# SiLU behind three weight copies, and one down piece split between the two halves of the gate

## The chip, the cores and the metric

The kernel runs on one core of one Trainium2 chip. Its time is that of one execution on the device in microseconds (us); lower is better. PE is the matrix engine (TensorE), DVE the vector engine (VectorE), ACT the scalar engine (ScalarE), POOL GpSimd, SP the queue that issues most DMAs.

## The reference, cut to what matters

One layer of a bidirectional encoder on 1024 tokens of width 1024: an adaLN norm, differential attention, then a mixture of 16 experts of width 512, of which each token uses two, and a last norm. The change lies in the experts:

```python
hid = silu(t @ w_gate) * (t @ w_up)      # per expert: 1024 -> 512, twice
hid = hid * gates                        # weight of the token for this expert
y = hid @ w_down                         # 512 -> 1024, summed over experts
x = x + g2 * y
```

## The kernel before, in words

Attention and routing fill the first part of the run. The experts e = 0 to 15 then follow one after the other, each in a call of `block`. An expert gathers its tokens. The first 128 go through the main path; if it has more, up to 64 further ones go through a second, smaller path (`small_gate`, `small_up`, `small_hid`, `small_down`), which stands under a branch at run time.

Float32 products are made of pairs: a value is kept as a high part (fp32r) and the rest (low), and a product is the sum of three matmuls, high x high, high x low and low x high. So each weight has to be split on chip. An expert's weights are 12 pieces of 128 x 1024 values: pieces 0 to 3 belong to the gate product, 4 to 7 to the up product, 8 and 9 to the first half of the down product, 10 and 11 to its second. A piece is loaded by a DMA on SP into one of 11 raw tiles, copied by ACT into its high part (`split_hi`, L1115), and DVE subtracts that from the raw piece to get the low part (`split_lo`, L1120). After the split the raw tile is free and the load of the piece 11 places later is issued (`split_done`, `raw_to`). High and low parts lie in a ring of 14 slots.

ACT, DVE, POOL and PE work in exactly the order in which the program names their instructions (`manual_schedule`). What stands beside the matmuls is put in place by hooks: a hook (c, what) is issued just before matmul number c of the block, and `upto(c)` issues all that are due by c. For experts 1 to 15 the list `SPL` sets pieces 4, 5 and 6 at c = 0, 8 and 16, and pieces 7, 8 and 9 at c = 24, 32 and 40. Expert 0 has pieces 8 to 11 in a list of its own (`SP0`), the last two at c = 30 and 40.

In a block, PE does the gate product (24 matmuls, c = 0 to 23), then the up product for the first 6 of 8 row groups (18 matmuls, c = 24 to 41), then the last two row groups in two halves of 256 columns (6 short matmuls each). ACT takes SiLU of the gate columns (`silu`, L1385). DVE multiplies SiLU, the token's weight and the up columns for each half (`gated`, L1391); the second half's matmuls wait for the first half's `gated`, since both halves lie in one PSUM tile. Eight small DVE instructions that build a one-hot matrix for expert e + 2 (L1228, hook c = 46) stand ahead of the first `gated`; experts 14 and 15 have none. Then PE transposes the next expert's tokens (L1274) and the gated columns (`hid`, L1428), ACT and DVE split these (L1431, L1432), and PE does the down product in two halves (L1441); the second half's transposes stand after six matmuls of the first. Before the change `splits(11)`, that is the split of piece 10, stands after the first `hid`, and pieces 11, 12 and 13 (the last two are the next expert's first two) follow by `splits(14)`, both ahead of the second `hid` on ACT and DVE.

Of the kernel before, what the change touches and what calls it, by code (L numbers as in the profile page):

```python
# [15 lines left out]
P = 128  # L16
S = 1024
D = 1024
KT = D // P
# [16 lines left out]
def build(tc, x, c, ada_w, ada_b, norm_mix, norm_ffn, w_in, lq1, lk1, lq2, lk2, subln, w_out,  # L36
# [1098 lines left out]
    def split_to(n):  # L1135
        while nsplit[0] < min(n, NE * NP):
            split_piece(*divmod(nsplit[0], NP))
            split_done(1)
# [143 lines left out]
    def small_pt():  # L1282
        return mps.tile([P, KT, M2], F32, name="xt", bufs=2)
# [13 lines left out]
    def run(g):  # L1297
        try:
            while True:
                next(g)  # L1300
        except StopIteration as r:
            return r.value
# [33 lines left out]
    def finish15(ix, py, yo, xc):  # L1336
        sq = ss_tile()
        for i in range(2):
            h = slice(i * 512, (i + 1) * 512)
            v.tensor_tensor(yo[:, h], py[i], g2b[:, h], op=OP.mult)  # L1340
            v.tensor_tensor(xc[:, h], xc[:, h], yo[:, h], op=OP.add)
            nc.scalar.activation(py[i], xc[:, h], AF.Square, accum_out=sq[:, i:i + 1])
            if i == 0:
                nc.scalar.activation(sq[:, 0:1], sq[:, 0:1], AF.Identity, scale=1.0 / D, bias=epst)
        v.tensor_tensor(yo, xc, nfin[0], op=OP.mult)
        r = sq[:, 1:2]
        nc.scalar.activation(r, r, AF.Ln, scale=1.0 / D, bias=sq[:, 0:1])
        nc.scalar.activation(r, r, AF.Exp, scale=-0.5)
        nc.scalar.activation(yo[:, 0:512], yo[:, 0:512], AF.Copy, scale=r)
        v.tensor_scalar(yo[:, 512:1024], yo[:, 512:1024], r, None, op0=OP.mult)  # L1350
        out_rows(ix, yo)
# [19 lines left out]
    def gu_tile():  # L1371
        return mps.tile([P, 512], F32, name="gu", bufs=2)

    def gu(e, XT, i, R, pg, ks=range(KT), n=slice(0, 512)):

        for k in ks:
            for xi, wi in TERMS[R]:
                yield
                w = WP[e, i * 4 + k // 2][wi].rearrange("p (k n) -> p k n", k=2)
                nc.tensor.matmul(pg[:, n], XT[:, xi, k], w[:, k % 2, n], start=(k == 0 and xi == 0 and wi == 0),  # L1380
                                 stop=(k == KT - 1 and (xi, wi) == TERMS[R][-1]), skip_group_check=True)

    def silu(pg):
        sl = mp.tile([P, 512], F32, name="sl")
        nc.scalar.activation(sl, pg, AF.Silu)  # L1385
        return sl

    def gated(sl, pu, g, hf):

        n = slice(hf * 256, hf * 256 + 256)  # L1390
        v.scalar_tensor_tensor(sl[:, n], sl[:, n], g, pu[:, n], op0=OP.mult, op1=OP.mult)  # L1391
        return sl[:, n]
# [32 lines left out]
    def hid(sl, R, name="hid", bufs=2, hT=None):  # L1425
        ph = mps.tile([P, 2, P], F32, name="tp")
        for i in range(2):
            nc.tensor.transpose(ph[:, i, :R], sl[:R, i * P:(i + 1) * P], ident[:R, :R])  # L1428
        hT = mp.tile([P, 2, 2, P], F32R, name=name, bufs=bufs) if hT is None else hT
        hi, lo = hT[:, 0], hT[:, 1]  # L1430
        nc.scalar.copy(hi, ph[:, :, :R])  # L1431
        v.tensor_tensor(lo, ph[:, :, :R], f(hi), op=OP.subtract)  # L1432
        return hT

    def down(e, py, hf, hT, R, ns=(0, 1)):
        terms = [(i, xi, wi) for i in range(2) for xi, wi in TERMS[R]]
        terms.sort(key=lambda t: t[1])
        for n in ns:
            for j, (i, xi, wi) in enumerate(terms):
                yield  # L1440
                nc.tensor.matmul(py[n], hT[:, xi, i], WP[e, 8 + hf * 2 + i][wi][:, n * 512:(n + 1) * 512],  # L1441
                                 start=(hf == 0 and j == 0), stop=(hf == 1 and j == len(terms) - 1), skip_group_check=True)

    def take(g, n):
        for _ in range(n):
            next(g, None)
# [25 lines left out]
    def small15(XT, ix, g):  # L1472

        e, R, xs = NE - 1, M2, XG[NE - 1, 1]
        small_evac(small_pe(xs), XT)
        xc = raw_tile()
        acc_rows(ix, xc[:R])
        small_gate(e, XT, gu_tile(), xs)
        small_up(e, XT, gu_tile(), xs, g)
        hs = mp.tile([P, 2, 2, P], F32R, name="hs")  # L1480
        small_hid(xs, hs)
        small_down(e, [mps.tile([P, 512], F32, name="spy%d" % n, tag="xt", bufs=2) for n in range(2)], hs, xs)
        xc, yo = xc[:R], xs[:R]
        v.tensor_tensor(xc, xc, yo, op=OP.add)
        sq = ss_tile()[:R]
        nc.scalar.activation(yo, xc, AF.Square, accum_out=sq[:, 0:1])
        r = rstd_of(sq, R)
        v.scalar_tensor_tensor(xc, xc, r, nfin[0][:R], op0=OP.mult, op1=OP.mult)
        out_rows(ix, xc)
# [28 lines left out]
    def block(e, XT, idx, tt, hooks):  # L1518


        count = [0]
        ix = idx[:, 0:1]
        last = e == NE - 1
        hooks = sorted(hooks, key=lambda hk: hk[0])
        py = [mps.tile([P, 512], F32, name="py%d" % i) for i in range(2)]

        def upto(c):
            while hooks and hooks[0][0] <= c:
                hooks.pop(0)[1]()

        def go(g, n=1 << 30):
            try:
                for _ in range(n):
                    next(g)
                    upto(count[0])
                    count[0] += 1
            except StopIteration as r:
                return r.value

        def splits(k):  # L1540

            split_to(e * NP + k)

        g1 = tt[:, 0, 1:2]
        pg, pu = gu_tile(), gu_tile()
        go(gu(e, XT, 0, P, pg))
        st = silu(pg)
        go(gu(e, XT, 1, P, pu, range(KT - 2)))
        sl = []
        for hf in range(2):  # L1550
            go(gu(e, XT, 1, P, pu, range(KT - 2, KT), slice(hf * 256, hf * 256 + 256)))
            sl.append(gated(st, pu, g1, hf))
        upto(99)
        if last:
            h0 = hid(sl[0], P)
            splits(NP)
            run(down(e, py, 0, h0, P))
            upto(150)
            h1 = hid(sl[1], P)
            nc.scalar.preload_act_table_set("natural_log_exp_and_others")  # L1560
            upto(1 << 30)
            run(down(e, py, 1, h1, P))
            finish15(ix, py, mp.tile([P, D], F32, name="yo"), XC[0])
            tc.no_sync_barrier()
            with tc.If(cnts[e] > P, label="small"):
                small15(XT, idx[:M2, 1:2], tt[:, 1, 1:2])
            tc.no_sync_barrier()
            with tc.If(cnts[NE] > P + M2):
                rest(XT)
            return  # L1570
        n = cnts[e]
        g = tt[:, 1, 1:2]
        xs = XG[e, 1]

        def small(what):
            tc.no_sync_barrier()
            with tc.If(n > P):  # L1577
                what()

        def evac():  # L1580
            yo = mp.tile([P, D], F32, name="yo")
            for n in range(2):
                v.tensor_tensor(yo[:, n * 512:(n + 1) * 512], py[n], g2b[:, n * 512:(n + 1) * 512], op=OP.mult)
            scatter_add(ix, yo)

        pt = small_pt()
        small(lambda: small_evac(small_pe(xs, pt), XT))

        upto(XPH)
        h0 = hid(sl[0], P)  # L1590

        upto(SMM)
        splits(11)
        sg, su = gu_tile(), gu_tile()
        small(lambda: small_gate(e, XT, sg, xs))
        splits(14)
        d = down(e, py, 0, h0, P)
        take(d, 6)
        h1 = hid(sl[1], P)
        run(d)  # L1600
        small(lambda: small_up(e, XT, su, xs, g))
        splits(15)
        run(down(e, py, 1, h1, P))
        if e == NE - 2:
            evac()
        hs = mp.tile([P, 2, 2, P], F32R, name="hs")
        spy = [mps.tile([P, 512], F32, name="spy%d" % n, tag="xt", bufs=2) for n in range(2)]

        def small_d():
            small_down(e, spy, hs, oyo)  # L1610
            scatter_add(idx[:M2, 1:2], oyo[:M2])

        small(lambda: small_hid(xs, hs))
        splits(16)
        later.append((DSM if e < NE - 2 else 4, lambda: small(small_d)))
        if e < NE - 2:
            later.append((EVAC, evac))
        upto(1 << 30)
# [14 lines left out]
    XT = run(xpose(XG[0, 0]))  # L1633
# [22 lines left out]
    for e in range(NE):  # L1656
# [46 lines left out]
        if e + 1 < NE:  # L1703
# [4 lines left out]
            XT = xp[0]  # L1708
# [34 lines left out]
```

## Time and profile before

| | before |
|---|---|
| median of 3 runs | 1269.76 us (1265.92 to 1269.80) |
| profiled execution, its own time | 1267.65 us |
| its span | 1265.9 us |
| mean granted TensorE clock | 0.945 of full speed |
| busy share of the span: PE, DVE, ACT, POOL | 89%, 74%, 57%, 20% |
| experts 0 to 14, SiLU of expert 0 to SiLU of expert 15 | 455.24 us |

Read a row of the timeline as: start in us from the span's start, duration in us, engine, line, operation, output and inputs, number of instructions merged into it, and in brackets how long the engine had been idle before it and what it waited for. "whi" and "wlo" are the high and low parts of a weight piece, "wraw" the raw piece, "gu" the PSUM tiles of gate and up, "sl" the SiLU tile, "py" the down product. A row of the windows view gives a stretch, its length, the busy us and number of instructions of PE, PE's weight loads, DVE, ACT and POOL, then the granted clock as a share of full speed (1.00 is 2.4 GHz, 0.50 is 1.2 GHz), the mean busy share of the DMA engines and what they moved in GB/s; its last line sums the stretches asked for. A matmul's duration includes what overlaps the next one; the starts give the rate.

### The profile page before, as it was taken

The page shows a single profiled execution, that of the slowest core. Times are in us where ns is not written, and L with a number is a line of the kernel's source. Part 1 is how long each engine was busy: PE and PEld are TensorE (multiplying, and loading weights), DVE is VectorE, ACT ScalarE, POOL GpSimd, SP SyncE. Part 2 cuts the span into 40 slices and gives each one's busy share as a digit, 9 for nine tenths or more (in the row PEclk, how much of TensorE's full clock was granted, in tenths as well). Part 3 has the DMA queues.
Part 4 walks back from the last instruction along what each step waited for, and adds up shares of the span by engine and source line. Part 5 has one row for each costly group of instructions (what it writes and reads, how often), then busy time and mean ns, then how long its engine had stood idle before and what let it go on. Part 6 is the DMA issues. An engine that isn't in the chain of part 4 may idle for free. (4 is left out here: it accounts for less than half of the span.)

```text
span 1265.9 us, 17489 instructions
## 1 busy us (share of the span) xinstructions
PE 1126.6 (89%) x5896; PEld 891.1 (70%) x5896; DVE 941.7 (74%) x1548; ACT 722.3 (57%) x1178; POOL 259.5 (20%) x250
## 2 busy tenths in 40 slices
PE   4989999999999999998999969888989888988990
PEld 3657777777777787776778857666767666777770
DVE  5868788898889677779755577767667778576774
ACT  5556766666677676767644235545455565454553
POOL 3011110111111020125024123212112223122122
PEclk8999999999999999998999979888989989898996
DMA  9622032323223110125058347877776878667745
GB/s 329 193 67 63 25 102 81 98 84 90 82 83 92 34 38 16 36 76 162 25 182 289 124 142 276 267 274 234 230 245 200 269 260 292 220 207 219 223 137 232
DMA packets 120479, 199.41 MB, mean 158 GB/s; under 512 B 12967, under 2 KB 58696, under 8 KB 120370
## 3 DMA queue, kind: packets, MB, share of 16 engines
q1 hardware_dynamic: 113664, 179.86, 42.2%
q0 software_dynamic: 6512, 17.68, 5.9%
q8 instruction: 53, 0.87, 0.3%
q10 hardware_dynamic: 194, 0.54, 0.2%
q14 instruction: 56, 0.46, 0.1%
HBM read 175.77 MB, written 27.67 MB: 161 GB/s over the span
## 5 line engine op out<-in xcount | busy, mean ns | idle before, releaser
L1120 DVE TENSOR_TENSOR wlo<-wraw,whi 128x1024 fp32r<-128x1024 f32 x187 | 224.2, 1234 | 63.2 <-ACT whi L1115 47.3
L1380 PE MATMUL gu<-whi,XT 128*128 128x512 f32 (+1 forms) x672 | 220.6, 391 | 32.8 <-DVE sl L1391 30.1
L486 ACT ACTIVATE E<-E,mn 128x1024 f32<-128x1024 f32 x128 | 147.1, 1151 | 85.1 <-DVE mn L483 84.6
L1115 ACT CAST whi<-wraw 128x1024 fp32r<-128x1024 f32 x192 | 191.5, 1046 | 6.4 <-DMA wraw<-in_expert_w_gate 1.4
L1380 PEld LDWEIGHTS gu<-whi,XT 128*128 128x128 f32 x672 | 128.9, 195 | 69.4 <-DVE sl L1391 33.3
L483 DVE CUSTOM_DVE_ANT_0 E<-S,negd 128x1024 f32<-128x1024 f32 x128 | 152.8, 1219 | 18.2 <-PE S L478 17.6
L1380 PE MATMUL gu<-wlo,XT 128*128 128x512 f32 (+1 forms) x384 | 149.5, 389 | 0.0
L285 PE MATMUL mm<-hH,wh 128*128 128x512 f32 x336 | 139.3, 415 | 2.1 <-DVE V L384 2.1
L285 PE MATMUL mm<-hL,wh 128*128 128x512 f32 x336 | 140.2, 417 | 0.0
L285 PE MATMUL mm<-hH,wl 128*128 128x512 f32 x336 | 138.8, 413 | 0.0
L143 POOL TENSOR_TENSOR wl<-wraw,wh 128x1024 fp32r<-128x1024 f32 x21 | 50.6, 2410 | 325.8 <-ACT wh L142 255.7
L513 ACT CAST aH<-tp 128x512 fp32r<-128x512 f32 x128 | 74.0, 578 | 72.8 <-PE tp L511 72.5
L1441 PE MATMUL py<-whi,hid 128*128 128x512 f32 x256 | 97.4, 434 | 14.8 <-ACTq L1577 5.8
L497 DVE SCALAR_TENSOR_TENSOR E<-E,r 128x1024 f32<-128x1024 f32 x64 | 85.8, 1340 | 27.8 <-ACT E L495 26.3
L514 DVE TENSOR_TENSOR aL<-tp,aH 128x512 fp32r<-128x512 f32 x128 | 87.9, 687 | 17.5 <-ACT aH L513 16.3
L511 PE MATMUL tp<-ident,E 128*128 128x128 f32 x512 | 78.8, 277 | 10.8 <-DVE aL L514 7.4
L511 PEld LDWEIGHTS tp<-ident,E 128*128 128x128 f32 x512 | 62.6, 142 | 34.3 <-DVE aL L514 14.4
L1380 PEld LDWEIGHTS gu<-wlo,XT 128*128 128x128 f32 x384 | 76.1, 198 | 14.6
L693 PE MATMUL mm<-wo,wh 128*128 128x512 f32 x240 | 80.0, 408 | 1.3 <-ACT mm L705 1.3
L285 PEld LDWEIGHTS mm<-hH,wh 128*128 128x128 f32 x336 | 63.5, 189 | 18.2 <-issue 5.1
L285 PEld LDWEIGHTS mm<-hH,wl 128*128 128x128 f32 x336 | 63.5, 189 | 17.1 <-issue 7.9
L285 PEld LDWEIGHTS mm<-hL,wh 128*128 128x128 f32 x336 | 63.3, 189 | 16.9 <-issue 8.0
(341 smaller groups left out, 2230.8 us busy)
## 6 DMA issues: line engine op xcount, KB each, us to landing
wraw<-in_expert_w_gate SPq DMA_DIRECT2D x64, 512.0 KB
wraw<-in_expert_w_up SPq DMA_DIRECT2D x64, 512.0 KB
wraw<-in_expert_w_down SPq DMA_DIRECT2D x64, 512.0 KB
aw<-in_ada_w SPq DMA_DIRECT2D x64, 256.0 KB
wraw<-in_attn_w_in SPq DMA_DIRECT2D x23, 512.0 KB
ld<-in_ada_w SPq DMA_DIRECT2D x32, 256.0 KB
ld<-in_x SPq DMA_DIRECT2D x8, 512.0 KB
xt<-in_x SPq DMA_DIRECT2D x8, 512.0 KB
```

The costliest lines, as they stand in the source:

```text
L285: nc.tensor.matmul(pq, w[:, k], t[k][:, n], start=(k == 0 and i == 0), stop=(k == KT - 1 and i == 2))
L483: nc.vector.tensor_tensor_reduce(out=e, in0=sps[m], in1=negd[:, w0:w0 + S], op0=OP.add, op1=OP.min, scale=-slope, scalar=3.0e38, accum_out=mn)
L486: nc.scalar.activation(e, e, AF.Exp, bias=mn, scale=-1.0, accum_out=sm)
L497: nc.vector.scalar_tensor_tensor(es[0], es[1], r2, es[0], op0=OP.mult, op1=OP.add)
L511: nc.tensor.transpose(pt[:, i], a[:, k * P:(k + 1) * P], ident)
L513: nc.scalar.copy(th[:, kk * 4:kk * 4 + 4, q], pt)
L514: nc.vector.tensor_tensor(tl[:, kk * 4:kk * 4 + 4, q], pt, f(th[:, kk * 4:kk * 4 + 4, q]), op=OP.subtract)
L693: nc.tensor.matmul(py, w[:, h], wt[h][:, ns], start=(h == 0 and s == 0), stop=(h == H - 1 and s == 2))
L1115: nc.scalar.copy(WP[e, i][0], RAW[e, i])
L1120: eng.tensor_tensor(low, RAW[e, i], f(high), op=OP.subtract)
L1380: nc.tensor.matmul(pg[:, n], XT[:, xi, k], w[:, k % 2, n], start=(k == 0 and xi == 0 and wi == 0), stop=(k == KT - 1 and (xi, wi) == TERMS ...
L1441: nc.tensor.matmul(py[n], hT[:, xi, i], WP[e, 8 + hf * 2 + i][wi][:, n * 512:(n + 1) * 512], start=(hf == 0 and j == 0), stop=(hf == 1 and ...
```

## The change

In the source, SiLU of the gate columns moves from ahead of the up product's first 18 matmuls to behind them. On PE nothing moves. On ACT, in experts 1 to 15, SiLU now stands behind the copies of pieces 7, 8 and 9; in expert 0 behind those of pieces 10 and 11. `upto(40)` issues nothing that was not issued already. The split of piece 10 moves from after the first `hid` to between the first and the second `gated`: its copy on ACT, its subtraction on DVE, and on SP the load of the piece 11 places later. In expert 0 piece 10 is split by then already.

```diff
@@ -1544,12 +1544,16 @@
         g1 = tt[:, 0, 1:2]
         pg, pu = gu_tile(), gu_tile()
         go(gu(e, XT, 0, P, pg))
+        go(gu(e, XT, 1, P, pu, range(KT - 2)))
+
+        upto(40)
         st = silu(pg)
-        go(gu(e, XT, 1, P, pu, range(KT - 2)))
         sl = []
         for hf in range(2):
             go(gu(e, XT, 1, P, pu, range(KT - 2, KT), slice(hf * 256, hf * 256 + 256)))
             sl.append(gated(st, pu, g1, hf))
+            if hf == 0:
+                splits(11)
         upto(99)
         if last:
             h0 = hid(sl[0], P)
@@ -1590,7 +1594,6 @@
         h0 = hid(sl[0], P)
 
         upto(SMM)
-        splits(11)
         sg, su = gu_tile(), gu_tile()
         small(lambda: small_gate(e, XT, sg, xs))
         splits(14)
```

## Rows read from the trace of the kernel before

**Rows 1.** Page: costliest groups; xcount, busy us, mean ns, idle before, releaser.
```profile
L1380 PE MATMUL gu<-whi,XT 128*128 128x512 f32 (+1 forms) x672 | 220.6, 391 | 32.8 <-DVE sl L1391 30.1
...
L1115 ACT CAST whi<-wraw 128x1024 fp32r<-128x1024 f32 x192 | 191.5, 1046 | 6.4 <-DMA wraw<-in_expert_w_gate 1.4
```
**Rows 2.** Windows, SiLU to SiLU, experts without second path (eight summed; 1 and 7 shown).
```profile
790.29:816.26 25.97, 22.93 (x108) 17.82 (x107) 19.75 (x28) 14.30 (x20) 7.24 (x8) 0.87 0.79 254
...
974.28:999.54 25.26, 20.35 (x108) 15.49 (x107) 19.96 (x29) 14.08 (x20) 8.81 (x10) 1.00 0.84 268
...
sum 210.00, PE 175.16 PEld 134.17 DVE 158.21 ACT 113.57 POOL 58.65; mean PE 21.90 PEld 16.77 DVE 19.78 ACT 14.20 POOL 7.33
```
**Rows 3.** Timeline, ACT, expert 1, around SiLU.
```profile
784.27 1.05 ACT L1115 CAST whi<-wraw 128x1024 fp32r<-128x1024 f32 x1 [0.20 <-ACTq L1577]
790.29 0.60 ACT L1385 ACTIVATE sl<-gu 128x512 f32<-128x512 f32 x1 [4.97 <-PE gu L1380]
790.79 2.94 ACT L1115 CAST whi<-wraw 128x1024 fp32r<-128x1024 f32 x3
```
**Rows 4.** Timeline, DVE, expert 1, from piece 6 to the second gated half.
```profile
787.92 1.23 DVE L1120 TENSOR_TENSOR wlo<-wraw,whi 128x1024 fp32r<-128x1024 f32 x1 [0.21 <-DVEq L1577]
791.86 3.50 DVE L1120 TENSOR_TENSOR wlo<-wraw,whi 128x1024 fp32r<-128x1024 f32 x3 [2.71 <-ACT whi L1115]
795.27 1.52 DVE L1228 TENSOR_SCALAR rk<-rk 128x192 bf16<-128x192 bf16 x8
796.71 0.48 DVE L1391 SCALAR_TENSOR_TENSOR sl<-sl,tt,gu 128x256 f32<-128x256 f32 x1
798.24 0.48 DVE L1391 SCALAR_TENSOR_TENSOR sl<-sl,tt,gu 128x256 f32<-128x256 f32 x1 [1.06 <-PE gu L1380]
```
**Rows 5.** Timeline, PE, first matmul of the up product's second half: experts 0, 1, 14.
```profile
774.05 0.38 PE L1380 MATMUL gu<-whi,XT 128*128 128x256 f32 x1 [0.95 <-DVE sl L1391]
...
797.24 0.38 PE L1380 MATMUL gu<-whi,XT 128*128 128x256 f32 x1 [2.15 <-DVE sl L1391]
...
1195.03 0.39 PE L1380 MATMUL gu<-whi,XT 128*128 128x256 f32 x1 [0.69 <-DVE sl L1391]
```
**Rows 6.** Timeline, DVE, expert 7.
```profile
975.85 3.50 DVE L1120 TENSOR_TENSOR wlo<-wraw,whi 128x1024 fp32r<-128x1024 f32 x3 [1.26 <-ACT whi L1115]
...
985.63 1.23 DVE L1120 TENSOR_TENSOR wlo<-wraw,whi 128x1024 fp32r<-128x1024 f32 x1 [0.18 <-ACTq L1577]
987.07 3.52 DVE L1120 TENSOR_TENSOR wlo<-wraw,whi 128x1024 fp32r<-128x1024 f32 x3 [0.21 <-DVEq L1577]
990.51 0.41 DVE L1432 TENSOR_TENSOR hid<-tp,hid 128x256 fp32r<-128x256 f32 x1
```
**Rows 7.** Timeline, ACT, expert 7, from piece 10 to the second hid.
```profile
984.54 4.12 ACT L1115 CAST whi<-wraw 128x1024 fp32r<-128x1024 f32 x4
988.56 0.36 ACT L1431 CAST hid<-tp 128x256 fp32r<-128x256 f32 x1
```
**Rows 8.** Timeline, PE, expert 7, down product.
```profile
984.61 0.50 PE L1441 MATMUL py<-whi,hid 128*128 128x512 f32 x1 [0.30 <-ACT hid L1431]
...
988.97 0.50 PE L1441 MATMUL py<-whi,hid 128*128 128x512 f32 x1 [1.08 <-ACTq L1577]
...
990.98 0.95 PE L1441 MATMUL py<-whi,hid 128*128 128x512 f32 x3 [0.81 <-DVEq L1577]
```
**Rows 9.** Windows, experts 4, 6, 11, 12, 13, with second path (12 and sum shown).
```profile
1116.64:1151.94 35.30, 31.83 (x168) 25.63 (x167) 25.48 (x39) 17.92 (x27) 7.85 (x9) 1.00 0.69 211
...
sum 189.23, PE 173.35 PEld 139.66 DVE 126.50 ACT 89.80 POOL 34.47; mean PE 34.67 PEld 27.93 DVE 25.30 ACT 17.96 POOL 6.89
```
**Rows 10.** Windows: expert 0, SiLU to SiLU.
```profile
768.24:790.29 22.05, 20.09 (x108) 15.54 (x107) 17.04 (x26) 11.26 (x16) 6.46 (x9) 1.00 0.84 311
```
**Rows 11.** Windows: 7 us of expert 1 behind its wait; expert 14.
```profile
799.00:806.00 7.00, 6.85 (x37) 5.70 (x36) 5.18 (x6) 6.09 (x11) 2.99 (x5) 0.51 0.30 104
...
1189.52:1223.48 33.96, 31.33 (x152) 24.89 (x151) 24.32 (x31) 17.75 (x26) 5.23 (x2) 1.00 0.52 143
```

## The prediction

> **What bounds the kernel now.** I read the costliest groups first, then windows cut from one SiLU to the next, then the timeline of PE, DVE and ACT inside such windows. The costliest group of PE, the gate and up matmuls, has 32.8 us of idle time ahead of it, and 30.1 of that ends with DVE's `gated` (L1391) [rows 1]: PE waits there, and the change works on just that place. The reader is to see next that the experts make 455.24 us of the span and come in two kinds: eight windows of 108 PE matmuls, 210.00 us together [rows 2], and five of 168 with the second path, 189.23 us [rows 9]; expert 0, with 22.05 us, is the shortest of all [rows 10], and expert 14 stands by itself [rows 11].
>
> Inside expert 1 the chain that ends last runs over three engines. ACT is through with the copy of piece 6 at 785.32, then stands idle 4.97 us, because its next instruction is SiLU and the gate product ends only at 790.29; behind it come the copies of pieces 7, 8 and 9 [rows 3]. DVE, free at 789.15, waits 2.71 us for the first of them, does the three subtractions until 795.36, the one-hots until 796.79 and `gated` until 797.19 [rows 4]. PE starts at 797.24 after 2.15 us of idle time, so it had been done at 795.09 [rows 5]. A second stall lies in the down product: in expert 7 PE waits 1.08 us for ACT's second `hid` and 0.81 us for DVE's [rows 8], which stand behind four copies and four subtractions [rows 6, 7].
>
> **Part 1: SiLU behind the three copies.** The copies can then start at about 785.4 and end at 788.3 (2.94 us [rows 3]), long before the gate ends, so SiLU itself is not later in such an expert. DVE does the subtractions from 789.15 on: 3.50 to 792.65, one-hots 1.52 to 794.17 [rows 4]. PE reaches the end of the first half at 795.09; so DVE is ready 0.9 us ahead of it, and what is late next is PE's own work. What stays is the way PE to DVE to PE: 0.48 for `gated` and about 0.2 to and fro. Expert 14, which has no one-hots, shows it as 0.69 us [rows 5]. Gain 2.15 - 0.69 = 1.46 us. In an expert that follows one with the second path, DVE waits only 1.26 us for the copies [rows 6]; there the gain is 1.26. ACT is later there too, and SiLU moves back; at worst the copies start where SiLU did (974.28) and SiLU ends at 974.28 + 2.94 + 0.60 = 977.82, still ahead of `gated` at 980.70 - 1.26 = 979.44 (980.70 being 975.85 + 3.50 + 1.52 less the overlaps of expert 1 [rows 4]).
>
> Sum of part 1: of the eight short windows two (experts 5 and 7) follow a second path, so 6 x 1.46 + 2 x 1.26 = 11.3; of the five long ones experts 12 and 13 do, so 3 x 1.46 + 2 x 1.26 = 6.9. Expert 0 waits 0.95 [rows 5] and its copies of pieces 10 and 11 move ahead: 0 to 0.26, taken 0.2. Expert 14 is at its 0.69 already: 0. Expert 15 has no row here; by one copy less of 1.05 [rows 1] ahead of its last norm 0 to 1.05, and I take 0.5. Together 18.9 us.
>
> **Part 2: piece 10 between the halves.** Removed from behind the first `hid`: one copy on ACT, one subtraction on DVE. In expert 7 four copies take 4.12 us ahead of the second `hid` [rows 7]; three end 1.03 earlier, and PE's wait of 1.08 shrinks to 0.05. On DVE the subtraction of piece 11 takes the place of piece 10's at 985.63, three of them end at 985.63 + 3.52 = 989.15, and `hid` follows until 989.5, where it ended at 990.92 [rows 6]. PE, which resumed at 990.98 [rows 8], resumes at 989.54: 1.44 us gained. Its four matmuls in between, 988.97 to 990.17, now end at 989.1, so a wait of 0.4 us on DVE stays.
>
> Added elsewhere: the copy (1.05) lies on ACT behind SiLU, where ACT has nothing until the next expert's tokens. The subtraction (1.23) lies on DVE between the two `gated`, where DVE idled 1.06 us for PE's second half [rows 4]. So the second `gated` comes 0.17 later; its reader is the second `hid`'s transposes behind six down matmuls, which hides that; without this cover it costs 0.17 each. SP's load for the piece 11 places later is asked for some 7 us earlier, in the same order; behind it wait only other loads. Cost 0.
>
> In the eight short windows the gain is 8 x 1.44 = 11.5. In the long ones PE does 60 more matmuls (168 against 108), the small gate right behind piece 10's old place; I find no wait of PE on the second `hid` to remove and take 0, with ends 0 and 6 x 1.44 = 8.6. In expert 0 piece 10 is done by then: 0.
>
> **Part 3: the clock.** This is no edit but follows from the first two. In expert 1, two us behind the wait, the clock stands at 0.51 for 7 us [rows 11], that is at 1.2 GHz; the same work costs more than in windows at 1.00. Against expert 7 (25.26 at clock 1.00) the eight short windows lose 210.00 - 8 x 25.26 = 7.9 us [rows 2], and against expert 12 (35.30 at 1.00) the five long ones lose 189.23 - 5 x 35.30 = 12.7 [rows 9]: 20.6 us in all. The fourteen experts beside 0 and 14 wait about 2.0 us each (30.1 less 0.95 and 0.69 [rows 1, 5]); some of them keep the clock (7 and 12) and others lose it. Experts 0 and 14, which wait under 1 us, keep it [rows 10, 11]. With no wait above 0.9 left, I take two thirds of the 20.6 as won: 13.7; the ends are 0 and 20.6.
>
> The Trainium skill speaks against this: "TensorE: Matmul & The Clock Gate", section "A second HAM failure mode: psum-queue depth-cycling", tells of a kernel whose matmul groups are parted by idle times so short that one would not mind them, and whose clock swings between the levels all the same. By that rule nothing of part 3 comes; experts 0 and 14 at 1.00 speak against it here, expert 1 for it.
>
> **Sum.** 18.9 + 11.5 + 13.7 = 44.1 us. The execution that the rows come from took 1267.65 us: 1223.5. The median of the runs stands 2.1 above that execution, so I forecast 1225 us, by itself 1216 to 1233. A check from another side: expert 0 has pieces 8 to 11 split ahead, waits 0.95, and its window is 22.05 us [rows 10]; my sum turns expert 7's 25.26 into 25.26 - 1.26 - 1.44 = 22.56.
>
> **The rivals.**
> - The waits go and the clock does not come back (the rule above as a mechanism of this kernel: the 0.7 us before the second half and the 0.4 us in the down product suffice for it to fall). Then only 30.4 us go: 1269.8 - 30.4 = 1239 us, 1233 to 1243. For it: long and short waits both stand in windows at 1.00, so the wait is not all.
> - DVE becomes the bound. Expert 7 keeps it busy 19.96 us [rows 2]; with five gaps of 0.2 behind branches and a wait of about 1.1 for the tokens it needs 22.1 of the 22.5 us that the sum leaves. If DVE stays behind by 1.5 us per short window, 8 x 1.5 = 12 us are lost again: 1237, and 1233 to 1248. For it: only 0.4 us of room; against it: one idle time of 2.71 and one of 1.06 are what is filled [rows 4].
> - Slower: SiLU now stands behind the copy of piece 9, so a raw piece 9 that lands late holds SiLU, `gated` and PE. It decides from the point where SiLU would end behind 796.71, the start of `gated` before; every us beyond costs 14 us over 14 experts. Three us beyond: 14 x 3 - 11.5 = 30 us, some 1300. Against it: 192 copies waited 6.4 us in all, at most 1.4 of it named for a DMA [rows 1], and in expert 0 the DMA moved 311 GB/s through a window of 22.05 us at a share of 0.84 [rows 10].
> - It does not do what it says: the copies of pieces 7 to 9 cannot start earlier, since their ring slots or raw tiles come free late; then part 2 alone is left, 1258, or nothing, 1270. Against it: the slots are those of pieces of the expert before, whose up product is long done.
>
> **How the numbers follow.** The forecast gets 0.55, the clock that stays low 0.20, DVE as the bound 0.13, no effect or part 2 alone 0.05, slower 0.04, and faster than 1216 (all of the clock, some gain in the long windows) 0.03. The range 1214 to 1243 holds the first, nearly all of the second and two thirds of the third: a little over 8 in 10. A change below 0.3% (3.8 us) can't be told from none here. Faster by more than that: the cases that end below 1266, 0.92; within it 0.04; slower 0.04.
>
> **What would show it.** Right: on ACT the copies of pieces 7 to 9 directly behind that of piece 6 and SiLU without a long wait ahead of three copies; PE's idle time on L1391 about 11 us in all instead of 30.1; the second `hid` behind three copies and PE's two waits in the down product near 0 and 0.4; short windows near 22.5 us; a granted clock above 0.945. Wrong: a wait of ACT's copies on a DMA, a `gated` that DVE reaches later than PE's first half ends by over 0.3 us, or windows at 0.87 clock as before.

## The result and the profile after

The changed kernel takes 1228.17 us (median of 4 runs, 1226.90 to 1231.08) against 1269.78 us (median of 4 runs, 1265.92 to 1273.82). The ratio is 0.9675, with a 95% interval of 0.964 to 0.9711: 3.2% faster, 3 us above the forecast of 1225. Ratios leave out a run that lies over 1.5% above the fastest of its kernel; that is one run of experiment 2, at 1272.47 us. The profiled execution took 1226.90 us with a span of 1225.0, so 40.8 us less than the one the prediction was made from; the mean granted clock rose from 0.945 to 0.963.

The two groups of [rows 1] after the change, and ahead of them DVE's subtractions, in the same columns:

```profile
L1120 DVE TENSOR_TENSOR wlo<-wraw,whi 128x1024 fp32r<-128x1024 f32 x187 | 222.5, 1231 | 24.0 <-ACT whi L1115 19.5
L1380 PE MATMUL gu<-whi,XT 128*128 128x512 f32 (+1 forms) x672 | 217.2, 386 | 14.2 <-DVE sl L1391 11.5
...
L1115 ACT CAST whi<-wraw 128x1024 fp32r<-128x1024 f32 x192 | 190.2, 1046 | 8.5 <-DVE rk L1674 2.7
```

PE's idle time that ends with `gated` fell from 30.1 to 11.5 us. The copies wait no more for DMAs than before: 0.9 us in all, against 1.4.

SiLU itself has moved, so windows are cut here at PE's first matmul of the up product's second half, the place of [rows 5]. First the span in three stretches (start to expert 0, experts 0 to 15, tail) of the kernel before, then of the changed one:

```profile
700.00:774.05 74.05, 61.71 (x377) 53.11 (x375) 50.99 (x113) 25.55 (x55) 16.69 (x23) 0.84 0.45 158
774.05:1228.98 454.93, 399.87 (x1934) 314.25 (x1934) 324.86 (x462) 233.33 (x329) 109.04 (x120) 0.92 0.73 234
1228.98:1265.90 36.92, 7.53 (x34) 5.58 (x34) 17.91 (x19) 15.86 (x29) 7.74 (x10) 0.69 0.64 254
```

```profile
700.00:774.29 74.29, 61.90 (x377) 53.13 (x376) 50.97 (x113) 25.89 (x56) 16.68 (x23) 0.84 0.45 158
774.29:1185.18 410.89, 377.80 (x1934) 295.96 (x1935) 321.74 (x463) 233.51 (x330) 103.28 (x119) 0.99 0.79 259
1185.18:1225.00 39.82, 8.94 (x34) 6.64 (x34) 17.79 (x19) 15.02 (x28) 7.45 (x11) 0.63 0.63 240
```

The experts gain 44.04 us at a clock of 0.99 against 0.92; the tail behind expert 15's second half loses 2.90. I had not forecast that loss; it has its own experiment below.

The changed kernel's experts without second path (expert 2, the second row shown, and the sum of the eight), to be held against [rows 2]; then experts 6 and 12 and the sum of the five with second path, against [rows 9]:

```profile
818.95:841.54 22.59, 20.37 (x106) 15.48 (x106) 19.46 (x29) 14.09 (x19) 6.64 (x8) 1.00 0.94 326
...
sum 180.85, PE 162.80 PEld 123.75 DVE 155.80 ACT 112.86 POOL 55.88; mean PE 20.35 PEld 15.47 DVE 19.47 ACT 14.11 POOL 6.98
...
923.60:957.53 33.93, 31.82 (x167) 25.64 (x167) 25.24 (x39) 17.92 (x27) 5.46 (x8) 1.00 0.75 241
...
1081.92:1117.36 35.44, 33.33 (x166) 26.84 (x167) 25.23 (x39) 17.98 (x27) 7.24 (x9) 0.95 0.69 213
...
sum 173.99, PE 163.58 PEld 131.74 DVE 124.77 ACT 89.74 POOL 31.98; mean PE 32.72 PEld 26.35 DVE 24.95 ACT 17.95 POOL 6.40
```

Cut in this way the kernel before has 209.98 and 187.81 us for the same experts. All eight short windows now stand at clock 1.00, and seven of them between 22.54 and 22.59 us (the other has 22.82); of the long ones three are at 1.00 and two (0.91, 0.95) are not.

In these two the low stretch does not follow `gated`. It begins behind another wait of PE, on the split of the second path's tokens (DVE, L1295), which the change left as it was. In expert 12 the matmuls behind it take 0.63 us instead of the usual 0.39:

```profile
1085.45 0.63 PE L1274 MATMUL xt<-ident,xgxa 128*128 128x128 f32 x4 [1.33 <-DVE XT L1295]
...
1087.47 0.63 PE L1380 MATMUL gu<-wlo,XT 128*128 128x512 f32 x1
```

In expert 4 the same wait of 1.33 us ends at 867.66, and the clock stands at 0.51 from 868 to 875. Experts 6, 11, 13 and 14 have it too and stay at 1.00. In the kernel before, PE's waits on this line were 0.88 to 1.33 us.

Inside a short expert (number 8) the timeline of the changed kernel shows the new order, first ACT, then DVE, then PE:

```profile
968.70 3.89 ACT L1115 CAST whi<-wraw 128x1024 fp32r<-128x1024 f32 x4 [0.19 <-ACTq L1581]
974.59 0.60 ACT L1385 ACTIVATE sl<-gu 128x512 f32<-128x512 f32 x1 [2.00 <-issue]
975.09 1.04 ACT L1115 CAST whi<-wraw 128x1024 fp32r<-128x1024 f32 x1
...
983.60 2.96 ACT L1115 CAST whi<-wraw 128x1024 fp32r<-128x1024 f32 x3
986.47 0.35 ACT L1431 CAST hid<-tp 128x256 fp32r<-128x256 f32 x1
```

```profile
977.09 1.52 DVE L1228 TENSOR_SCALAR rk<-rk 128x192 bf16<-128x192 bf16 x8
979.53 0.48 DVE L1391 SCALAR_TENSOR_TENSOR sl<-sl,tt,gu 128x256 f32<-128x256 f32 x1 [0.91 <-PE gu L1380]
979.93 1.22 DVE L1120 TENSOR_TENSOR wlo<-wraw,whi 128x1024 fp32r<-128x1024 f32 x1
981.07 0.48 DVE L1391 SCALAR_TENSOR_TENSOR sl<-sl,tt,gu 128x256 f32<-128x256 f32 x1
...
984.69 3.50 DVE L1120 TENSOR_TENSOR wlo<-wraw,whi 128x1024 fp32r<-128x1024 f32 x3 [0.41 <-ACT whi L1115]
988.10 0.42 DVE L1432 TENSOR_TENSOR hid<-tp,hid 128x256 fp32r<-128x256 f32 x1
```

```profile
980.07 0.39 PE L1380 MATMUL gu<-whi,XT 128*128 128x256 f32 x1 [0.67 <-DVE sl L1391]
...
983.44 0.50 PE L1441 MATMUL py<-whi,hid 128*128 128x512 f32 x1 [0.30 <-ACT hid L1431]
986.87 0.50 PE L1441 MATMUL py<-whi,hid 128*128 128x512 f32 x1 [0.16 <-ACTq L1581]
988.58 0.95 PE L1441 MATMUL py<-whi,hid 128*128 128x512 f32 x3 [0.50 <-DVEq L1581]
```

ACT copies pieces 6 to 9 in one go, then waits 2.00 us for SiLU and copies piece 10 right behind it. DVE now waits for PE ahead of the first `gated` (0.91 us) where PE waited for DVE, and the subtraction of piece 10 fills the time ahead of the second `gated`, which follows with no wait named. PE's wait ahead of the second half is 0.67 us, its two in the down product 0.16 and 0.50 (1.08 and 0.81 in [rows 8]).

### The profile page after: what moved, and what is told of

Its sections match the earlier page's. It is cut to its first block, busy times and chain, and to the rows that moved or that the text cites. A ratio compares the mean times of both kernels' runs of the same rounds, so it can differ in the third digit from the quotient of the medians.

```text
span 1225.0 us, 17508 instructions
## 1 busy us (share of the span) xinstructions
PE 1107.5 (90%) x5896; PEld 874.3 (71%) x5896; DVE 937.4 (77%) x1548; ACT 721.8 (59%) x1178; POOL 253.0 (21%) x250
## 5 line engine op out<-in xcount | busy, mean ns | idle before, releaser
L1120 DVE TENSOR_TENSOR wlo<-wraw,whi 128x1024 fp32r<-128x1024 f32 x187 | 222.5, 1231 | 24.0 <-ACT whi L1115 19.5
L1380 PE MATMUL gu<-whi,XT 128*128 128x512 f32 (+1 forms) x672 | 217.2, 386 | 14.2 <-DVE sl L1391 11.5
L1441 PE MATMUL py<-whi,hid 128*128 128x512 f32 x256 | 92.7, 415 | 11.3 <-ACT hid L1431 5.6
```

The source lines that it names most:

```text
L1120: eng.tensor_tensor(low, RAW[e, i], f(high), op=OP.subtract)
```

## The experiments

Theory A was that of the prediction: two separate stalls of PE, each paid once per expert, and a clock that comes back when the wait on `gated` goes. Its rivals were that only one part of the change counts, and that the clock hangs on other waits.

**1. SiLU alone.** Piece 10 is split at its old place. The edits of experiments 1 to 4 are shown against the changed kernel, cut to the lines that differ.

```diff
             sl.append(gated(st, pu, g1, hf))
-            if hf == 0:
-                splits(11)
...
         upto(SMM)
+        splits(11)
```

> SiLU behind the copies of pieces 7 to 9, piece 10 split at its old place. Theory A (each wait costs by itself, and the clock is held by the short wait ahead of the up product's second half): PE's idle time on the gated halves about 11.5 us as in the changed kernel, the two waits of about 1.1 and 0.8 us in the down product back in the eight short experts, 8 x 1.22 = 10 us above the changed kernel: about 1238. Rival B (either stall lets the clock fall): short experts at 0.87 to 0.94 of the clock again, up to 15 us more: about 1250. Rival C (the SiLU move does all, the split nothing): 1228.

Measured: 1241.90 us (ratio to the kernel before 0.9788, 0.9751 to 0.9825), 13.7 above the changed kernel, with a granted clock of 0.960 to 0.964. PE's idle time on `gated` is 11.5 us again, and the two waits of the down product are back, here in expert 8 of this kernel:

```profile
989.06 0.50 PE L1441 MATMUL py<-whi,hid 128*128 128x512 f32 x1 [0.30 <-ACT hid L1431]
993.44 0.51 PE L1441 MATMUL py<-whi,hid 128*128 128x512 f32 x1 [1.10 <-ACTq L1579]
995.44 0.96 PE L1441 MATMUL py<-whi,hid 128*128 128x512 f32 x3 [0.81 <-DVEq L1579]
```

Rival C is out: the split is worth something by itself. From the start of the down product PE resumes 6.38 us later here and 5.14 us later in the changed kernel, 1.24 us per short expert or 10 us for eight.

The clock is nearly kept: over the runs it is as high as in the changed kernel, and seven of the eight short windows are at 1.00, with both these waits back and only the wait on `gated` short. The eighth, that of expert 1, loses it: cut at the first `gated` it takes 25.26 us at 0.93, the others 23.79 to 23.89. There it falls right behind the two waits of the down product; the three matmuls of the second row take 1.37 us instead of 0.96:

```profile
803.45 0.50 PE L1441 MATMUL py<-whi,hid 128*128 128x512 f32 x1 [1.11 <-ACTq L1579]
805.46 1.37 PE L1441 MATMUL py<-whi,hid 128*128 128x512 f32 x3 [0.81 <-DVEq L1579]
```

So Rival B holds for one window of eight. Of the 13.7 us, 10 are the two waits; the rest, expert 1's clock among it, was not taken apart.

**2. The split alone.** SiLU stands where it stood.

```diff
         go(gu(e, XT, 0, P, pg))
+        st = silu(pg)
         go(gu(e, XT, 1, P, pu, range(KT - 2)))
-
-        upto(40)
-        st = silu(pg)
```

> Piece 10 between the two halves, SiLU at its old place. Theory A: PE's wait of about 2.1 us ahead of the second half is back in 13 experts (18.6 us) and with it most of the clock loss (15 us), while the tail is short as in the kernel before (3 us less): about 1258. If the clock holds in spite of the 2.1 us waits (Rival B: it was the waits in the down product that let it fall): about 1244. If the split moves nothing (Rival C): 1270.

Measured: 1259.25 us (median of seven runs; ratio 0.9904, 0.9869 to 0.994), as Theory A has it, but the single runs spread more than those of any other kernel here, and they lie nearly in the order of their clock:

```
us       1249.55  1251.85  1252.15  1259.25  1260.41  1261.24  1272.47
clock      0.956    0.953    0.953    0.944    0.942    0.944    0.929
```

Its profile, taken from the fastest of these runs, shows a cause. The windows are those of experts 1, 2 and 3 of this kernel, cut at the first `gated`:

```profile
795.61:821.58 25.97, 22.95 (x106) 18.02 (x106) 19.56 (x29) 14.29 (x19) 5.79 (x8) 0.87 0.83 286
821.58:845.61 24.03, 20.33 (x106) 15.47 (x106) 19.46 (x30) 14.08 (x19) 6.65 (x8) 1.00 0.87 293
845.61:869.63 24.02, 20.30 (x106) 15.46 (x106) 19.47 (x29) 14.09 (x19) 6.67 (x8) 1.00 0.89 297
```

At full clock such a window takes 24.02 us, 1.43 more than the 22.59 of the changed kernel: that is the wait of 2.1 us against 0.67 by itself. With the clock at 0.87 it takes 1.94 us more. With this wait in place some windows lose the clock and some keep it, and the mean clock changes from run to run. All five low stretches among the experts of this profile begin at the wait ahead of the second half or within 2 us of its end. In the kernel before, eight of ten do; the other two (experts 2 and 5) begin behind the waits of the down product, as expert 1's does in experiment 1. So most of the clock loss hangs on the wait ahead of the second half, but the waits in the down product can cost the clock too. What makes it fall in one window and not in the next is not shown by these runs.

**3. The tail.** In the last expert alone SiLU goes back.

```diff
         go(gu(e, XT, 0, P, pg))
+        if last:
+            st = silu(pg)
         go(gu(e, XT, 1, P, pu, range(KT - 2)))
...
-        st = silu(pg)
+        if not last:
+            st = silu(pg)
```

> The changed kernel, but in expert 15 alone SiLU stands where it stood before. From the up product's second half of expert 15 to the end the changed kernel takes 39.8 us against 36.9 before. Theory D (five subtractions in a row on DVE hold up GpSimd's scatter of expert 14's rows, 4.08 us against 1.43, and the loads of the accumulated rows wait for it): the scatter takes about 1.4 us again, the loads start about 2.7 us earlier against the second half, and the time is 2 to 3 us below the changed kernel: about 1225.5. Rival (the tail is longer for another reason, such as DMA traffic): 1228.

Measured: 1226.62 us (ratio 0.9668, 0.9631 to 0.9706). The time alone decides nothing, 1.5 us below the changed kernel; the rows do. Expert 14's scatter on POOL, DVE beside it, and the first load of the accumulated rows on SP, in the changed kernel:

```profile
1179.91 4.08 POOL L1455 DMA_INDIRECT accd<-oyo,ix  x1 [5.37 <-DVE wlo L1120]
...
1176.93 5.75 DVE L1120 TENSOR_TENSOR wlo<-wraw,whi 128x1024 fp32r<-128x1024 f32 x5
...
1186.08 3.96 SPq L1355 DMA_DIRECT2D wraw<-accd  x8
```

and in this one:

```profile
1180.31 1.43 POOL L1455 DMA_INDIRECT accd<-oyo,ix  x1 [5.48 <-DVE wlo L1120]
...
1181.55 3.50 DVE L1120 TENSOR_TENSOR wlo<-wraw,whi 128x1024 fp32r<-128x1024 f32 x3 [1.99 <-ACT whi L1115]
...
1183.89 4.58 SPq L1355 DMA_DIRECT2D wraw<-accd  x8
```

The copies that no longer wait for SiLU let DVE run its five subtractions without a gap, to 1182.68, and the scatter ends only 1.31 us behind the last of them. With the old gap of 1.99 us it takes 1.43 and the loads start 2.2 us earlier, in spite of a scatter that starts 0.4 later. The loads start 2.1 to 2.2 us after the scatter's end in both kernels, and in the one before. Theory D holds for the scatter and the start of the loads. It explains a part of the tail only: from expert 15's second half to the end it is 38.1 us here, against 39.8 in the changed kernel and 36.9 before. The last of ACT's eight norm sums starts at 1200.76 here, having waited 2.34 us for its load, and at 1200.90 in the changed kernel; why this load lands late is not shown.

**4. No wait between the halves.** The wait that stays, 0.67 us, comes from the halves' sharing one PSUM tile. DVE has room ahead of the first `gated`, so piece 10's split goes there, and PE need not stop between the halves.

```diff
         for hf in range(2):
             go(gu(e, XT, 1, P, pu, range(KT - 2, KT), slice(hf * 256, hf * 256 + 256)))
+        splits(11)
+        for hf in range(2):
             sl.append(gated(st, pu, g1, hf))
-            if hf == 0:
-                splits(11)
```

> The changed kernel with both halves of the up product's last two row groups ahead of the first gated, and piece 10 split ahead of it. PE no longer waits for DVE between the halves (11.5 us in all). Theory: DVE idles 1.2 to 2 us ahead of the first gated now, so the subtraction of piece 10 fits there, and PE gains 0.67 per expert: about 1218. Rival (DVE is as busy as PE, so the time comes back as a wait for the first gated or the first hid): 1226 to 1230.

Measured: 1219.04 us (1216.93 to 1222.16; ratio 0.9613, 0.9574 to 0.9652); every run lies below the changed kernel's fastest, 1226.90. The theory holds. The scatter in the tail is held up longer still, because DVE now has six subtractions in a row:

```profile
1168.76 5.25 POOL L1455 DMA_INDIRECT accd<-oyo,ix  x1 [5.31 <-DVE wlo L1120]
...
1165.82 6.89 DVE L1120 TENSOR_TENSOR wlo<-wraw,whi 128x1024 fp32r<-128x1024 f32 x6
```

They end at 1172.71 and the scatter at 1174.01, 1.30 behind them.

**5. The changed kernel again**, beside the two that follow, with no edit.

> The changed kernel once more, on the chip of the two kernels beside it, so that these can be compared with it. All theories: 1226 to 1231.

Measured: 1228.24 us (1227.24 to 1229.29; ratio 0.9671, 0.9644 to 0.9698).

**6. Both.** Experiments 3 and 4 together, with the edits of both.

> Both halves ahead of the first gated, and SiLU early in expert 15 alone. Theory (the two gains add: 9 us from PE's wait, 1.5 us from the scatter, more where the scatter took 5.25 us): 1216 to 1217.5, the scatter at 1.4 us. Rival (the last load of the accumulated rows lands no earlier, so the tail keeps its length): 1219, as without the early SiLU.

Measured: 1216.49 us (1214.33 to 1217.64; ratio 0.9572, 0.9544 to 0.96), 11.8 us below the changed kernel on the same chip. The scatter takes 1.43 us. This is the fastest kernel of the study.

**7. Piece 11 as well.** One edit on top of experiment 6:

```diff
-        splits(11)
+        splits(12)
         for hf in range(2):
             sl.append(gated(st, pu, g1, hf))
```

> As the kernel beside it, but piece 11 too is split ahead of the first gated. DVE idles about 1.15 us there in the short experts; the second hid then stands behind two copies and two subtractions, and PE's waits of 0.21 and 0.50 us in the down product go. Theory: gated comes 0.1 us later, which the transposes hide; 8 x 0.65 = 5 us less: about 1212. Rival (DVE is the bound, its work is only moved): same as the kernel beside it, within 2 us, with a new wait of PE ahead of the gated columns' transposes.

Measured: 1227.46 us (1221.59 to 1229.50; ratio 0.9669, 0.9642 to 0.9697): 11 us slower than experiment 6, neither what the theory nor what its rival had. Six of the eight short experts did gain, 21.42 to 21.72 us per window against 21.97 to 22.35. A good part of the loss is where I had not looked: in the experts that follow one with the second path, DVE has four instructions more (L1452, L1423) and no room for a second subtraction. There the transposes of the next expert's tokens wait until both `gated` are through, here in expert 5, DVE and then PE:

```profile
891.44 1.51 DVE L1228 TENSOR_SCALAR rk<-rk 128x192 bf16<-128x192 bf16 x8
892.87 2.35 DVE L1120 TENSOR_TENSOR wlo<-wraw,whi 128x1024 fp32r<-128x1024 f32 x2
895.14 0.87 DVE L1391 SCALAR_TENSOR_TENSOR sl<-sl,tt,gu 128x256 f32<-128x256 f32 x2
...
896.21 0.63 PE L1274 MATMUL xt<-ident,xgxa 128*128 128x128 f32 x4 [1.95 <-DVEq L1584]
```

In experiment 6 the same row has a wait of 0.80:

```profile
897.27 0.63 PE L1274 MATMUL xt<-ident,xgxa 128*128 128x128 f32 x4 [0.80 <-DVEq L1584]
```

With the long wait the clock went down too: 0.952 to 0.960 over the runs, against 0.964 to 0.967 in experiment 6. In the profiles the windows of experts 5 and 7, cut at the first `gated`, take 23.90 and 23.93 us at 0.86 against 21.99 and 21.96 at 1.00. The long experts lose as well: expert 6 takes 34.63 us against 33.49, at 1.00 in both. The profile of this kernel is of its fastest run, 4 us above that of experiment 6, so it does not show all of the 11 us, and wait and clock were not taken apart.

## Why the prediction was right

**Part 1 held.** PE's idle time on `gated` was to go from 30.1 to about 11 us and went to 11.5. DVE was to be ready 0.9 us ahead of PE in an expert of the common kind; it waits 0.91. PE keeps 0.67 us where 0.69 was read off expert 14 (1.00 in expert 1). The waits before were not 2.0 us in fourteen experts, but 2.12 to 2.15 in thirteen and 0.70 in expert 15. In the four experts behind a second path PE had waited as long as elsewhere (2.12 to 2.14 us) and keeps 0.76 to 0.78, so the gain is 1.36 where 1.26 was read from DVE's wait. One window stands at full clock in both kernels, from expert 7's second half to expert 8's, first before, then after:

```profile
981.23:1006.48 25.25, 20.32 (x107) 15.46 (x107) 19.65 (x28) 14.08 (x19) 7.72 (x10) 1.00 0.88 285
```

```profile
957.53:980.07 22.54, 20.31 (x107) 15.49 (x107) 19.47 (x29) 14.10 (x19) 7.97 (x10) 1.00 0.97 316
```

It holds expert 7's down product and expert 8's wait on `gated`. It shrank by 2.71 us; by the prediction's terms it was to be 1.46 + 1.44 = 2.90, and the waits themselves say 1.47 (2.14 to 0.67) + 1.23.

**Part 2 held, a little oversized.** PE's wait on ACT went to 0.16 (0.05 forecast), that on DVE to 0.50 (0.4). From the start of the down product PE resumes after 5.14 us, where 4.93 was forecast and 6.37 stood [rows 8]: 1.23 instead of 1.44 us. The missing 0.2 is that the subtractions of pieces 11 to 13 start 1.25 us after the down product's start, and piece 10's did 1.02 after it [rows 6, 8]; I had let piece 11 take that very place, but its copy, too, now starts later, 0.16 us behind the product's first matmul instead of 0.07 ahead of it. So part 2 gave 8 x 1.23 = 9.8 us instead of 11.5. Experiments 1 and 2 show that the two parts can be had one by one.

**Part 3 held in size, but one premise did not.** Two thirds of 20.6 us, 13.7, were taken; no row gave that share. Of the 44.04 us, 18.6 are part 1's and 9.8 part 2's by the waits; about 15.6 are left for the clock. That part 2 came out 1.7 us smaller and the clock about 2 us larger, so that the sum fits to half a us, is luck. All eight short windows now stand at 1.00. Experiment 1 keeps nearly all of this clock and experiment 2 loses most of it, so it came back through part 1 in the main. "No wait above 0.9 left" was wrong: the waits of 1.33 us on the second path's tokens (L1295) were there before and stay. Both windows that are still below 1.00 lose the clock behind such a wait, and so do the five windows of this kind in the profiles of experiments 3 and 5. The rule of the Trainium skill that was weighed as a rival ("TensorE: Matmul & The Clock Gate", section "A second HAM failure mode: psum-queue depth-cycling"), that short idle times suffice for the clock to swing, does not describe the eight short windows with their 0.67, 0.16 and 0.50 us. Experiment 4 has one short window that may be such a case: expert 7's, 22.69 us at 0.92, falls behind waits of 0.30, 0.81 and 0.20 us. The same waits in experiment 6 left it at 1.00.

**DVE was not the bound**, though it came near: of 22.6 us it is busy 19.5. Experiment 7 shows the edge: one more subtraction in the same place is too much for the experts behind a second path.

**The step that failed is the tail.** I put expert 15 at 0 to 1.05 us of gain and took 0.5; the tail lost 2.9 us. I had counted ACT's copies there and not asked what a DVE without gaps does to POOL: the scatter took 4.08 us instead of 1.43. Experiment 3 gives 1.7 of the 2.9 us back; the cause of the other 1.2 stays open. So the forecast came out 3 us low, while the experts' 44.04 us stood against 43.6 forecast.

## What to carry to other kernels

An instruction that waits for a long product should stand behind everything on its in-order engine that does not need that product; the gain is read from the idle time of the engine behind it, and it ends where another engine becomes the late one (here PE, for which DVE now waits 0.91 us). A shorter stall can bring the clock back as well: price the same window at both clocks, from windows that show both, and list every wait that stays, not only the one that is cut. And when gaps on DVE close, look at what POOL did in them.

## What the runs showed of the hardware that was not expected

POOL's scatter of the second path's rows by indirect DMA takes 1.43 to 1.47 us by itself, and is held up by DVE subtractions (both inputs in SBUF) that run already: five in a row make it 4.08 us, six 5.25, and it ends 1.31 and 1.30 us behind the last of them. The nine profiles together have 54 of these scatters. The 24 that start while a subtraction runs end 1.31 to 1.36 us (once 1.44) behind the row that runs then. The other 30 take 1.43 to 1.47 us, even where a subtraction begins 0.1 us after them; one alone, in experiment 7, takes 3.74, and it starts 0.04 us ahead of two subtractions. The Trainium skill ("SBUF — State Buffer", section "Who interferes with whom") says that a DVE instruction with two SBUF inputs contends with a GpSimd instruction that reads SBUF; the rows agree with their 4.08 and 5.25 us. The same section infers that such an instruction does not delay the writing of DMA descriptors; here the indirect DMA that POOL issues is delayed, by as long as DVE's row of subtractions goes on.

The clock can be a matter of chance at the same work: with a wait of about 2.1 us in thirteen of the sixteen experts, experiment 2 ran at 0.929 to 0.956 and took 1249.55 to 1272.47 us, while the changed kernel, with 0.67 us in most, stayed within 4.2 us (1226.90 to 1231.08) and in experiment 5 within 2.1.
